# A decoder block on one core: the output projection ended row block by row block, the first up block put in another order, and the first chunk's operand sums written by transfers

## The chip, the core and the metric

The kernel runs on one core of a Trainium2 chip. The metric is the device time of one execution in microseconds (us). The engines are called as in the profile: PE (TensorE, matrix products), DVE (VectorE), ACT (ScalarE), POOL (GpSimd) and SP (SyncE, which only issues transfers here). POOL issues transfers too, the adding ones among them.

## The reference, cut to what matters

One decoder layer over 512 rows of width 2048, in float32. The parts that the change touches come after the two token mixers:

```python
y = jnp.concatenate([_rmsnorm(y_gm, gm_out_g[l]), _rmsnorm(y_lru, lru_out_g[l])], axis=-1)
x = x + jnp.einsum('bse,ed->bsd', y, w_out[l])            # output projection
h = _rmsnorm(x, norm2_g[l])
up = jnp.einsum('bsd,df->bsf', h, ffn_w_up[l])            # 2048 -> 2 * 6144
up = _causal_dwconv(up, ffn_conv_w[l], ffn_conv_b[l])     # width 3
gate, val = jnp.split(up, 2, axis=-1)
x = x + jnp.einsum('bsf,fd->bsd', jax.nn.gelu(gate) * val, ffn_w_down[l])
```

## The kernel before

**Products.** Every float32 operand is held as a rounded part and a rest (`h` and `l`); a product is three matmuls, h·h, h·l and l·h. `split` (L125) makes the pair: ACT casts (L126), DVE subtracts (L127). The up and down projections use Strassen's scheme in Winograd's form: an operand of 2x2 quarters gets seven slots, three of them quarters and four of them sums of quarters, and seven products replace eight. A unit (one weight operand against one activation operand) is 7 products of 6 matmuls (L854), in the order 1, 2, 6, 5, 3, 7, 4; `SLOTS` says which slots a product reads: products 1 and 2 read activation slots 6 and 4, products 6 and 5 slots 1 and 2, the rest 0, 3 and 5.

**Operands.** `stream` is the list in which operands are prepared: `Weights` and `Acts`, each with `load` (a transfer by SP, or transposes from rows), `sums` (three DVE instructions: L646 to L648 for weights, L672 to L674 for activations) and `pair` (the split). `prepare(upto)` writes these steps out in order: for each operand the load of the next, the sums of the next, its own pair, the load of the one after. For some weights ("made" ones: the first eight units and those around each chunk's start) the sums are made ahead in memory by adding transfers from POOL, spread over the kernel by `make` (L315), and `Weights.load` fetches them in place of the DVE sums. Raw operands lie in three rotating buffers `q` (a fourth is opened within the first down block), so a load waits for the pair of the operand three places before it. `ready(u)` says how far the list must be prepared before unit u.

**Stages around the change.** The output projection (`out_proj`, L556) runs over four column blocks d of 512 and, for each, over 8 steps of 128 in two halves, each half in two weight chunks; the four row blocks st of 128 rows have a bank of PSUM each and are taken in turn at every step, so that all four end together. Then DVE adds each to x (L569), `squares2` (L608) sends the rows to memory and squares them on ACT, `rms_rstd` (L224) makes the factor with 12 small DVE instructions for all rows, and `scale_rows` (L737) multiplies: column blocks 0 and 1 by DVE, 2 and 3 by ACT. From here on every engine's queue runs in the order in which the code writes it (L820). 40 idle products (L825) follow, then the first two activation operands: `from_rows` (L745) transposes two column tiles of 128 of x on PE into one bank (`tr`), ACT carries each into `q` (L753), and sums and pair follow. Operand m of the first up block holds column tiles 2m and 2m+1.

**Up blocks.** `up_block` (L882) runs 24 times (12 column groups, gate and value), 8 units each. In the first one the activations of the next units are transposed between the products: one tile when the operand is loaded, the other after the unit's third product. At the block's end `combine` (L867) makes the four output quarters from the seven banks, in one ACT copy and seven DVE instructions (L871 to L878); the next block's products take banks as these free them. After the first block the pools `tr` (1 bank) and `ps` (7 banks) are closed and one of 8 banks is opened. Convolution (L913, L918), gelu (L927), the product gate by value (L921) and the transfer to memory (`ad`, L923) are spread over the next block's units.

**Down blocks.** `down_block` (L947) reads `ad` back as activations, in chunks of 8, 8 and 6 operands; each chunk runs 4 blocks, one for each column block of the output. The operands of a chunk are spread in `stream` over the last units before it and its first units. At a block's end DVE and ACT carry the banks off (L971 to L978). A tail of plain products, `last_a` and `last_w`, ends the kernel.

Of the kernel before, what the change touches and what calls it, by code (L numbers as in the profile page):

```python
# [8 lines left out]
F32 = mybir.dt.float32  # L9
# [5 lines left out]
P = 128  # L15
# [63 lines left out]
def hybrid_block(ctx: ExitStack, tc: tile.TileContext, x, xT, w_in, w_out, w_up, w_dn, w_m4, w_dl, wab, wsT, vec, bs, vgb, fg, out):  # L79
# [235 lines left out]
    def make(n, after=None):  # L315
# [3 lines left out]
        for _ in range(min(n, len(to_make))):  # L319
            add, dst, src = to_make.pop(0)  # L320
            how = {"accum_op": ALU.add} if add else {}
            nc.gpsimd.dma_start(dst, src, max_dma_last_dim=8192, **how)  # L322
# [233 lines left out]
    def out_proj(d, half, ysrc, rstd, x_in, between=None):  # L556
        ps = [bank() for _ in range(NS)]
        for c in range(2):
            parts = wchunk(w_out[d, half * 2 + c])
            for i, wt in enumerate(parts):  # L560
                for kk in range(2):
                    e = c * 4 + i * 2 + kk
                    for st in range(NS):
                        mm3(ps[st], cols(ysrc[e], st), sl(wt, slice(None), kk, slice(None)), e == 0, e == NH - 1)
# [3 lines left out]
        for st in range(NS):  # L568
            nc.vector.scalar_tensor_tensor(x_in[:, st], ps[st], rstd[:, st:st + 1], x_in[:, st], ALU.mult, ALU.add)  # L569
# [38 lines left out]
    def squares2(d):  # L608
        nc.gpsimd.dma_start(x2d[d], x2[d])
        for st in range(NS):  # L610
# [46 lines left out]
    class Acts:  # L657


        def __init__(self, m, src=None, fill=None):  # L660
            self.m, self.src, self.fill = m, src, fill

        def load(self):
            self.q = slots("q")
            if self.fill is None:
# [4 lines left out]
        def sums(self):  # L670
            q = self.q
            nc.vector.tensor_tensor(q[:, 2:4], q[:, 7:8].broadcast_to([P, 2, 256]), q[:, 5:7], ALU.subtract)  # L672
            nc.vector.tensor_tensor(q[:, 1], q[:, 6], q[:, 2], ALU.subtract)
            nc.vector.tensor_tensor(q[:, 0], q[:, 4], q[:, 1], ALU.subtract)  # L674

# [61 lines left out]
    def scale_rows(d):  # L737
        for st in range(NS):
# [5 lines left out]

    def from_rows(m):  # L745

        def turn(q, kk):
            k = 2 * m + kk
            ps = pools["tr"].tile([P, S], F32, name="tr", tag="tr")
# [10 lines left out]
        def fill(q):  # L760
            turn(q, 0)
            halves.append(lambda: turn(q, 1))
# [7 lines left out]
    for c, s in zip(CHUNKS, starts):  # L770
        for i, p in enumerate(c):
            after.setdefault(s - 8 + spread[i] + 3, []).append(Acts(i, src=ad[p]))
# [29 lines left out]

    for d in range(4):
        if d == 3:
            prepare(place[2], place[2])
        out_proj(d, 0, ygm, rstd_g, x2[d], lambda c: squares2(d - 1) if d and c == 0 else None)
    squares2(3)
    rstd2 = const.tile([P, NS], F32, name="rstd2")
    rms_rstd(rstd2, ss2, D, NS)
    scale_rows(0)  # L810
# [13 lines left out]
    idle = pools["tr"].tile([P, S], F32, name="tr", tag="tr")  # L824
# [298 lines left out]
```

## Time and profile before

| | |
|---|---|
| time, median of 3 runs | 2063.87 us (2063.66 to 2065.06) |
| the profiled execution's own time | 2063.26 us |
| its span in the trace | 2061.6 us |
| PE, DVE, ACT, POOL busy | 2033.9, 1730.7, 904.3, 418.7 us |
| output projection ends, first product of the up blocks | 559.31, 574.28 us |
| first chunk's operands loaded | from 1514 us |

A row of a timeline gives the start, the duration, the engine, the line, what is written from what, and in brackets the idle time of that engine before the instruction with what ended it. A row of the table by stage gives the stretch, its length, each engine's busy time with the number of its instructions, the granted clock of PE (1.00 is full), the busy share of the transfer engines and what they moved in GB/s. Matmuls overlap, so their starts, not their durations, give the pace: 6669 in 800 us in an undisturbed stretch, or 0.120 us each. In a group of instructions the figures behind the bar are busy time, mean nanoseconds, and idle time before with its cause.

### The profile page before, as it was taken

How to read it: one execution, taken by the hardware profiler on the slowest of the kernel's cores; microseconds unless marked ns; L12 is line 12 of the kernel's file. 1: busy time of each engine (PE TensorE's matmuls, PEld its weight loads, DVE VectorE, ACT ScalarE, POOL GpSimd, SP SyncE). 2: the span in 40 equal slices, each digit the busy share in tenths (PEclk: the TensorE clock that was granted, in tenths of full speed). 3: DMA queues.
4: the chain of work that ended last, by engine and by line, in shares of the span. 5: the costliest groups of instructions: out<-in, count | busy, mean ns of one | idle time of the engine just before them, and what ended most of it. 6: DMA issues, size and time to landing. Idle time of an engine off the chain costs nothing.

```text
span 2061.6 us, 35459 instructions
## 1 busy us (share of the span) xinstructions
PE 2033.9 (99%) x14528; PEld 1920.2 (93%) x14528; DVE 1730.7 (84%) x2183; ACT 904.3 (44%) x887; POOL 418.7 (20%) x702
## 2 busy tenths in 40 slices
PE   9999999999989999999999999999999999999998
PEld 7888888888889999999999999999999999999996
DVE  7598882644379999999999999999989979879986
ACT  6445322423274444444444444444455345445443
POOL 0332233211222222222222222222211000000001
PEclk9999999999999999999999999999999999999999
DMA  7666687666435566656555655565556568558573
GB/s 244 185 170 165 176 208 178 179 188 203 139 120 161 164 160 177 172 154 179 167 156 172 167 169 172 161 172 159 154 206 214 189 224 277 184 196 285 175 245 138
DMA packets 105907, 376.39 MB, mean 183 GB/s; under 512 B 14608, under 2 KB 22160, under 8 KB 91792
## 3 DMA queue, kind: packets, MB, share of 16 engines
q1 hardware_dynamic: 65808, 246.30, 35.5%
q0 software_dynamic: 39360, 127.17, 25.6%
q8 instruction: 113, 1.85, 0.4%
q10 hardware_dynamic: 576, 0.66, 0.1%
q14 instruction: 50, 0.41, 0.1%
HBM read 341.57 MB, written 110.36 MB: 219 GB/s over the span
## 4 chain that ended last, share of the span: by engine, by line
PE 93%; DVE 4%; DMA 1%; ACT 1%; issue 0%; SPq 0%; DVEq 0%; ACTq 0%
PE qs L854 64%; PE ps L162 9%; PE ps L164 9%; PE ps L163 9%; DVE wl L127 1%; DMA q<-ad 1%; PE qs L163 1%; PE qs L164 1%; PE qs L162 1%; DVE al L127 1%; PE tr L751 0%; PE ps L582 0%; ACT wh L126 0%; DVE q L672 0%; DMA wraw<-w_in 0%
## 5 line engine op out<-in xcount | busy, mean ns | idle before, releaser
L854 PE MATMUL qs<-ah,wh 128*128 128x256 f32 x2688 | 762.7, 284 | 2.1 <-DVE pad L871 1.8
L854 PE MATMUL qs<-al,wh 128*128 128x256 f32 x2688 | 761.5, 283 | 0.0
L854 PE MATMUL qs<-ah,wl 128*128 128x256 f32 x2688 | 761.5, 283 | 0.0
L126 ACT CAST wh<-q 128x1792 fp32r<-128x1792 f32 (+1 forms) x282 | 476.7, 1691 | 640.1 <-PE qs L854 459.6
L127 DVE TENSOR_TENSOR wl<-q,wh 128x1792 fp32r<-128x1792 f32 (+1 forms) x282 | 567.7, 2013 | 54.2 <-ACT wh L126 53.6
L854 PEld LDWEIGHTS qs<-ah,wh 128*128 128x128 f32 x2688 | 516.8, 192 | 2.5 <-DVE pad L871 2.0
L854 PEld LDWEIGHTS qs<-al,wh 128*128 128x128 f32 x2688 | 516.8, 192 | 0.2 <-DVE al L127 0.2
L854 PEld LDWEIGHTS qs<-ah,wl 128*128 128x128 f32 x2688 | 516.8, 192 | 0.0
L854 PE MATMUL qs<-wh,ah 128*128 128x256 f32 x1232 | 350.4, 284 | 5.7 <-DVE xs L972 2.6
L854 PE MATMUL qs<-wl,ah 128*128 128x256 f32 x1232 | 349.8, 284 | 0.0
L854 PE MATMUL qs<-wh,al 128*128 128x256 f32 x1232 | 349.7, 284 | 0.0
L318 POOL COPY pace<-wl 128x1 f32<-128x1 f32 x236 | 125.8, 533 | 975.5 <-DVE wl L127 965.5
L127 DVE TENSOR_TENSOR wl<-wraw,wh 128x1024 fp32r<-128x1024 f32 (+2 forms) x105 | 117.9, 1125 | 150.6 <-ACT wh L126 145.7
L854 PEld LDWEIGHTS qs<-wh,ah 128*128 128x128 f32 x1232 | 237.6, 193 | 6.9 <-DVE xs L972 3.0
L854 PEld LDWEIGHTS qs<-wl,ah 128*128 128x128 f32 x1232 | 237.6, 193 | 0.1
L854 PEld LDWEIGHTS qs<-wh,al 128*128 128x128 f32 x1232 | 237.6, 193 | 0.0
L322 POOL DMA_DIRECT2D made<-w_m x324 | 232.1, 842 | 15.8 <-issue 15.7
L126 ACT CAST wh<-wraw 128x1024 fp32r<-128x1024 f32 (+2 forms) x105 | 102.1, 974 | 274.6 <-PE ps L163 142.6
L646 DVE TENSOR_TENSOR q<-q 128x512 f32<-128x512 f32 x226 | 154.5, 684 | 2.7 <-DMA q<-w_dn 2.6
L162 PE MATMUL ps<-xgh,wh 128*128 128x512 f32 x384 | 152.1, 397 | 0.7 <-ACT wh L126 0.7
L163 PE MATMUL ps<-xgl,wh 128*128 128x512 f32 x384 | 151.6, 395 | 0.0
L164 PE MATMUL ps<-xgh,wl 128*128 128x512 f32 x384 | 150.0, 395 | 0.0
(242 smaller groups left out, 2499.4 us busy)
## 6 DMA issues: line engine op xcount, KB each, us to landing
q<-w_up SPq DMA_DIRECT2D x176, 512.0 KB, 3.5
made<-w_m POOLq DMA_DIRECT2D x270, 256.0 KB, 5.0
wraw<-w_in SPq DMA_DIRECT2D x28, 1024.0 KB, 6.1
q<-made SPq DMA_DIRECT2D x54, 512.0 KB, 3.7
q<-w_dn SPq DMA_DIRECT2D x50, 512.0 KB, 3.6
wraw<-w_out SPq DMA_DIRECT2D x16, 1024.0 KB, 6.1
q<-w_dn SPq DMA_DIRECT2D x38, 384.0 KB, 4.5
ad<-gate POOLq DMA_DIRECT2D x48, 256.0 KB, 3.5
```

The costliest lines, as they stand in the source:

```text
L126: nc.scalar.copy(h, src)
L127: nc.vector.tensor_tensor(l, src, h.bitcast(F32), ALU.subtract)
L162: nc.tensor.matmul(ps, lhsT=ah, rhs=bh, start=start, stop=False)
L163: nc.tensor.matmul(ps, lhsT=ah, rhs=bl, start=False, stop=False)
L164: nc.tensor.matmul(ps, lhsT=al, rhs=bh, start=False, stop=stop)
L318: nc.gpsimd.tensor_copy(pace, after)
L322: nc.gpsimd.dma_start(dst, src, max_dma_last_dim=8192, **how)
L646: nc.vector.tensor_tensor(q[:, 2:4], q[:, 5:7], q[:, 7:8].broadcast_to([P, 2, 256]), ALU.add)
L854: nc.tensor.matmul(q[p][:, t], lhsT=x_, rhs=y_, start=first and t == 0 and n == 0, stop=last and t == 1 and n == 2, skip_group_check=True)
```

## The change

**The projection's end.** For the last column block (d = 3) the second weight chunk's steps are sorted by row block: a row block's four steps follow one another, and as it ends, `add(st)` and `norm2(st)` follow for it alone: squares on ACT, a square root on ACT, one reciprocal and four small DVE instructions, then `scale_rows` for column blocks 0 and 1 (block 1 of the last row block comes later). The sums of squares of column blocks 0 to 2 are added beforehand (`part2`), and `squares2(2)` moves ahead of that call.

**The first up block.** Idle products are 24, 8 and 8, in a bank of the other pool. Both column tiles of operands 0 and 1 are transposed at once, into two banks. Operand 0 is split in two pieces (`parts`): slots 4 to 6 need no sums. Later operands' transposes come after a unit's second and fifth product. At a block's last unit less is prepared ahead of `combine`, the rest after it; the down blocks likewise.

**The first chunk.** Its operands' sums are written to memory by 40 transfers from POOL, 5 for each of 8 operands, one at every second unit from the eleventh block on (`sum_up`). They can only add, so two quarters of each are stored negated (the gate product becomes two half instructions), and the signs are taken back where the banks are carried off (`plus`). Such an operand is loaded as 512 KB of sums and 384 KB of quarters in place of 512 KB, and has no DVE sums. The first chunk's `ad` is laid out quarter by quarter.

```diff
--- before.py
+++ after.py
@@ -312,12 +312,12 @@
...
-    def make(n, after=None):
+    def make(n, after=None, todo=to_make):
...
-        for _ in range(min(n, len(to_make))):
-            add, dst, src = to_make.pop(0)
+        for _ in range(min(n, len(todo))):
+            add, dst, src = todo.pop(0)
@@ -553,20 +553,30 @@
...
-    def out_proj(d, half, ysrc, rstd, x_in, between=None):
+    def out_proj(d, half, ysrc, rstd, x_in, between=None, in_turn=None):
...
+        def add(st):
+            nc.vector.scalar_tensor_tensor(x_in[:, st], ps[st], rstd[:, st:st + 1], x_in[:, st], ALU.mult, ALU.add)
...
-            for i, wt in enumerate(parts):
-                for kk in range(2):
-                    e = c * 4 + i * 2 + kk
-                    for st in range(NS):
-                        mm3(ps[st], cols(ysrc[e], st), sl(wt, slice(None), kk, slice(None)), e == 0, e == NH - 1)
+            todo = [(c * 4 + i * 2 + kk, sl(wt, slice(None), kk, slice(None)), st) for i, wt in enumerate(parts) for kk in range(2) for st in range(NS)]
+            turns = in_turn is not None and c == 1
+            if turns:
+                todo.sort(key=lambda t: t[2])
+            for e, w, st in todo:
+                mm3(ps[st], cols(ysrc[e], st), w, e == 0, e == NH - 1)
+                if turns and e == NH - 1:
+                    add(st)
+                    in_turn(st)
...
-        for st in range(NS):
-            nc.vector.scalar_tensor_tensor(x_in[:, st], ps[st], rstd[:, st:st + 1], x_in[:, st], ALU.mult, ALU.add)
+        if in_turn is None:
+            for st in range(NS):
+                add(st)
@@ -605,9 +615,14 @@
...
-    def squares2(d):
-        nc.gpsimd.dma_start(x2d[d], x2[d])
-        for st in range(NS):
+    ap, sums_of = ([tc.dram_tile([4, P, 256], F32, name=f"{n}{i}") for i in CHUNKS[0]] for n in ("ap", "as"))
+    for i in CHUNKS[0]:
+        ad[i] = ap[i].rearrange("s p c -> p s c")
+    def squares2(d, sts=range(NS)):
+        if NS - 1 in sts:
+            nc.gpsimd.dma_start(x2d[d], x2[d])
+        for st in sts:
@@ -657,21 +672,35 @@
...
-        def __init__(self, m, src=None, fill=None):
-            self.m, self.src, self.fill = m, src, fill
+        def __init__(self, m, src=None, fill=None, made=None):
+            self.m, self.src, self.fill, self.made = m, src, fill, made
...
-            if self.fill is None:
+            if self.made is not None:
+                nc.sync.dma_start(self.q[:, 0:4], self.made.rearrange("s p c -> p s c"))
+                nc.sync.dma_start(self.q[:, 4:7], self.src[:, 0:3])
+            elif self.fill is None:
...
+            if self.made is not None:
+                return
...
+        def parts(self):
+            act[self.m] = self.hl = act_tiles(self.m, [P, 7, 256])
+            (h, l), q = self.hl, self.q
+            nc.scalar.copy(h[:, 4:7], q[:, 4:7])
+            self.sums()
+            nc.vector.tensor_tensor(l[:, 4:7], q[:, 4:7], h[:, 4:7].bitcast(F32), ALU.subtract)
+            split(h[:, 0:4], l[:, 0:4], q[:, 0:4])
@@ -734,19 +763,23 @@
...
-    def scale_rows(d):
-        for st in range(NS):
+    def scale_rows(d, sts=range(NS)):
+        for st in sts:
...
+    def qbank():
+        return pools["ps"].tile([P, S], F32, name="qs", tag="qs")
...
-            ps = pools["tr"].tile([P, S], F32, name="tr", tag="tr")
+            ps = qbank() if m < 2 and kk else pools["tr"].tile([P, S], F32, name="tr", tag="tr")
@@ -758,8 +791,7 @@
...
-            turn(q, 0)
-            halves.append(lambda: turn(q, 1))
+            halves.extend((lambda: turn(q, 0), lambda: turn(q, 1)))
@@ -769,7 +801,7 @@
...
-            after.setdefault(s - 8 + spread[i] + 3, []).append(Acts(i, src=ad[p]))
+            after.setdefault(s - 8 + spread[i] + 3, []).append(Acts(i, src=ad[p], made=sums_of[i] if c is CHUNKS[0] else None))
@@ -800,14 +832,34 @@
...
+    rstd2 = const.tile([P, NS], F32, name="rstd2")
+    part2 = mx.tile([P, NS], F32, name="part2")
+    def norm2(st):
+        squares2(3, [st])
+        c = slice(st, st + 1)
+        v, y, u = (mx.tile([P, 1], F32, name=f"n2{n}", tag=f"n2{n}", bufs=2) for n in "vyu")
+        nc.vector.tensor_scalar(v, ss2[:, st, 3:4], 1.0 / D, part2[:, c], ALU.mult, ALU.add)
+        nc.scalar.activation(y, ss2[:, st, 3:4], AF.Sqrt, bias=part2[:, c], scale=1.0 / D)
+        nc.vector.reciprocal(y, y)
+        nc.vector.scalar_tensor_tensor(u, y, -0.5, y, ALU.mult, ALU.mult)
+        nc.vector.tensor_tensor(u, u, v, ALU.mult)
+        nc.vector.scalar_tensor_tensor(rstd2[:, c], u, 1.5, y, ALU.add, ALU.mult)
+        scale_rows(0, [st])
+        if st < NS - 1:
+            scale_rows(1, [st])
...
-        out_proj(d, 0, ygm, rstd_g, x2[d], lambda c: squares2(d - 1) if d and c == 0 else None)
-    squares2(3)
-    rstd2 = const.tile([P, NS], F32, name="rstd2")
-    rms_rstd(rstd2, ss2, D, NS)
-    scale_rows(0)
+        if d == 3:
+            with tc.high_priority(offset=AHEAD):
+                squares2(2)
+                nc.vector.tensor_reduce(part2, ss2[:, :, 0:3], mybir.AxisListType.X, ALU.add)
+                nc.vector.tensor_scalar(part2, part2, 1.0 / D, RMS_EPS, ALU.mult, ALU.add)
+        out_proj(d, 0, ygm, rstd_g, x2[d], lambda c: squares2(d - 1) if d in (1, 2) and c == 0 else None, norm2 if d == 3 else None)
@@ -821,25 +873,27 @@
...
-    idle = pools["tr"].tile([P, S], F32, name="tr", tag="tr")
-    for _ in range(40):
-        nc.tensor.matmul(idle[:, 0:256], lhsT=stream[0].hl[0][:, 0, 0:P], rhs=stream[0].hl[0][:, 1], start=True, stop=True)
+    idle = qbank()
+    def idle_products(n):
+        for _ in range(n):
+            nc.tensor.matmul(idle[:, 0:256], lhsT=stream[0].hl[0][:, 0, 0:P], rhs=stream[0].hl[0][:, 1], start=True, stop=True)
...
+    idle_products(24)
...
-    stream[first].sums()
-    scale_rows(1)
-    stream[first].pair()
+    idle_products(8)
+    stream[first].parts()
+    scale_rows(1, [NS - 1])
...
+    idle_products(8)
...
-    def qbank():
-        return pools["ps"].tile([P, S], F32, name="qs", tag="qs")
@@ -882,11 +936,13 @@
...
-            prepare(ready(u0 + m))
-            for p in ORDER:
+            prepare(ready(u0 + m) if m < 7 else min(ready(u0 + m), place[u0 + m + (2 if u0 else 1)]))
+            for n, p in enumerate(ORDER):
...
-                if p == 6:
-                    rest_of_loads()
+                if n in (1, 4) and halves:
+                    halves.pop(0)()
+            if u0 >= 80 and m % 2:
+                make(1, todo=sum_up)
@@ -897,6 +953,7 @@
...
+        prepare(ready(u0 + 7))
@@ -918,7 +975,12 @@
...
-                nc.vector.tensor_tensor(gate, gate, dst, ALU.mult)
+                if 2 * g + n in CHUNKS[0]:
+                    for t in (slice(0, 256), slice(256, 512)):
+                        nc.vector.scalar_tensor_tensor(gate[:, t], gate[:, t], -1.0 if (t.start == 0) == (j == 1) else 1.0, dst[:, t], ALU.mult, ALU.mult)
+                else:
+                    nc.vector.tensor_tensor(gate, gate, dst, ALU.mult)
@@ -936,6 +998,19 @@
...
+    sum_up = []
+    for k in range(len(CHUNKS[0]) + 3):
+        for r in range(4):
+            if 0 <= k - r < len(CHUNKS[0]):
+                dst, src = (t.rearrange("s (a b) c -> s a (b c)", b=8) for t in (sums_of[k - r], ap[k - r]))
+                sum_up += [
+                    [(0, dst[0:2], src[0:3:2]), (0, dst[2:4], src[1:3])],
+                    [(1, dst, src[3:4].broadcast_to([4, 16, 2048]))],
+                    [(1, dst[0:2], src[1:2].broadcast_to([2, 16, 2048]))],
+                    [(1, dst[0], src[2])],
+                ][r]
@@ -949,7 +1024,8 @@
...
-            prepare(ready(u0 + m))
+            ends = m == size - 1 and u0 + m + 3 < len(units)
+            prepare(min(ready(u0 + m), place[u0 + m + 2]) if ends else ready(u0 + m))
@@ -965,23 +1041,25 @@
...
+        plus = ALU.subtract if ci == 0 else ALU.add
...
-        tt(X11, X11, q[2], ALU.add)
+        tt(X11, X11, q[2], plus)
...
-        tt(X12, X12, q[3], ALU.add)
+        tt(X12, X12, q[3], plus)
...
-            lambda: tt(c5, c5, c6, ALU.add),
+            lambda: tt(c5, c6, c5, plus),
...
-            lambda: tt(c6, c6, c7, ALU.add),
+            lambda: tt(c6, c6, c7, plus),
...
-            lambda: tt(c5, c5, c7, ALU.add),
+            lambda: tt(c5, c5, c7, plus),
@@ -990,6 +1068,7 @@
...
+        prepare(ready(u0 + size - 1))
...
```

## The prediction

> **What bounds the kernel now.** I read the table by stage first, then PE's own idle times, then what the other engines do at those places.
>
> ```profile
> span 2061.6 us, 35459 instructions
> 700.00:1500.00 800.00, 800.00 (x6669) 800.00 (x6668) 766.72 (x973) 361.72 (x299) 207.84 (x357) 1.00 0.59 166
> 1500.00:1640.00 140.00, 135.40 (x1101) 0.98 0.61 211
> 1960.00:1990.00 30.00, 28.85 (x241) 1.00 0.58 192
> 574.60:578.40 3.80, 3.80 (x20) 3.80 (x19) 1.96 (x3) 2.27 (x2) 0.00 (x0) 0.50 0.54 197
> ```
>
> In the long middle PE never waits: 6669 matmuls in 800 us, 8.336 per us, 0.120 us each. There only fewer matmuls would help, and the change removes none. DVE is at 766.72 of 800 us (96%), so it bounds wherever it gets more work. At 1500 to 1640, 1101 matmuls need 132.1 us: 7.9 us are lost. At 1960 to 1990 it is 1.1 us. At 574.6 the clock is at half.
>
> PE's timeline at these places:
>
> ```profile
> 558.69 0.39 PE L163 MATMUL ps<-wl,ygmh 128*128 128x512 f32 x1
> 558.92 0.39 PE L164 MATMUL ps<-wh,ygml 128*128 128x512 f32 x1
> 559.47 5.06 PE L826 MATMUL tr<-wh 128*128 128x256 f32 x40 [0.16 <-DVE x L569]
> 571.62 1.11 PE L751 MATMUL tr<-ident,x 128*128 128x128 f32 x4 [3.35 <-ACT q L753]
> 574.28 0.56 PE L854 MATMUL qs<-ah,wh 128*128 128x256 f32 x1
> 586.38 0.66 PE L751 MATMUL tr<-ident,x 128*128 128x128 f32 x4 [1.77 <-ACT q L753]
> 600.19 0.65 PE L751 MATMUL tr<-ident,x 128*128 128x128 f32 x4 [1.78 <-ACT q L753]
> 628.39 0.39 PE L854 MATMUL qs<-ah,wh 128*128 128x256 f32 x1 [1.82 <-DVE pad L871]
> 631.87 0.36 PE L854 MATMUL qs<-ah,wh 128*128 128x256 f32 x1 [0.30 <-DVE v L877]
> 1558.98 0.58 PE L854 MATMUL qs<-wh,ah 128*128 128x256 f32 x1 [2.40 <-ACT c L870]
> 1607.01 0.39 PE L854 MATMUL qs<-wh,ah 128*128 128x256 f32 x1 [1.45 <-DVE xs L972]
> 1981.38 0.38 PE L854 MATMUL qs<-wh,ah 128*128 128x256 f32 x1 [1.15 <-DVE xs L972]
> ```
>
> Between the projection's end (559.31) and the first product (574.28) lie 15 us with 16 useful transposes, at most 0.66 us for four by the rows below 574.28. After the 3.35 us wait the clock is halved; it was halved after the wait of 2.40 us too, not after 1.82. The second up block's first unit has 12 matmuls left at 631.87 and ends at 633.3; I use that mark below.
>
> **The change, part by part.**
>
> *From the projection to the first product.* What sets it now, on DVE and ACT:
>
> ```profile
> 544.17 1.23 DVE L127 TENSOR_TENSOR wl<-wraw,wh 128x1024 fp32r<-128x1024 f32 x1 [4.17 <-ACT wh L126]
> 557.31 2.79 DVE L569 SCALAR_TENSOR_TENSOR x<-ps,rstd_g,x 128x512 f32<-128x512 f32 x4 [11.91 <-PE ps L164]
> 560.95 0.17 DVE L229 TENSOR_REDUCE rms_v<-ss 128x4 f32<-128x16 f32 x1 [0.85 <-ACT sq L612]
> 563.35 1.67 DVE L741 TENSOR_SCALAR x<-x,rstd 128x512 f32<-128x512 f32 x4
> 566.88 0.69 ACT L753 ACTIVATE q<-tr,vc 128x512 f32<-128x512 f32 x1 [0.75 <-PE tr L751]
> 567.60 0.69 DVE L672 TENSOR_TENSOR q<-q 128x512 f32<-128x512 f32 x1 [2.58 <-ACT q L753]
> 571.02 2.02 DVE L127 TENSOR_TENSOR al<-q,ah 128x1792 fp32r<-128x1792 f32 x1 [0.22 <-ACT ah L126]
> 583.20 2.55 ACT L743 ACTIVATE x<-x,rstd 128x512 f32<-128x512 f32 x4
> 618.61 2.02 DVE L127 TENSOR_TENSOR al<-q,ah 128x1792 fp32r<-128x1792 f32 x1
> 2023.04 1.28 ACT L1040 ACT_TABLE_LOAD   x1
> 2054.07 0.30 ACT L1040 ACTIVATE r3y<-ss,part 128x1 f32<-128x1 f32 x1
> 2054.99 0.16 DVE L1045 SCALAR_TENSOR_TENSOR r3r<-r3u,r3y 128x1 f32<-128x1 f32 x1
> ```
>
> Sorted steps need both halves of the last weights at once. They are ready at 545.4, and the last chunk (48 matmuls of 0.23 us, the step from 558.69 to 558.92) starts at 548.4: covered by 3 us, else up to 3 us would show. A row block now takes 2.7 us of PE and some 2.5 us of DVE (add 0.75, five small ones of 0.16 to 0.2, two scalings of 0.42), so only the last shows. The square root brings a table load of 1.28 us, and the next gelu another; ACT is 45% busy there and hides both. The new root's chain stands at the kernel's end: 1.1 us from the root's start (2054.07) to the factor (2055.15).
>
> Last row block: added at 560.1, squared at 560.95, factor at 562.1, scaled at 562.5 (now 565.0). If its add queues behind the scalings of the block before, all this is 0.8 us later. I take half. The 24 idle products (0.127 us each) start between 559.4 and 561.0, as their bank is or isn't the one that the last add reads; with the add, at 560.2, they end at 563.2. Eight transposes one after another, some 0.11 us each: 564.1. The second tile carried into `q`: 565.2. Sums (1.54 us): 566.8. The rests of slots 4 to 6, three sevenths of 2.02 us: 567.7. First product at 567.8, 6.5 us earlier. PE's waits on this way are under 1 us, so the clock stays, which saves 2.0 us (some 20 matmuls at 0.21). Together 8.5 us.
>
> *The first block gives part back.* I walked the queues instruction by instruction with these durations. The old order gives 632.1 for the mark at 633.3, without the half clock, and waits of 1.9 where the profile has 1.77 and 1.78. In the new order a unit's second transpose, after the fifth product, waits for ACT, which carried nothing off while it scaled column blocks 2 and 3 (2.55 us after a cast): 1.3 us in unit 0, 1.9 in units 1 and 3. DVE, whose sums begin only 2.4 us earlier (565.2 against 567.6), ends the last activation's rest at 615.7, where 618.61 + 2.02 = 620.6 stands now; PE waits 2.0 us for it. The second block's second product waits 2.1 us for `combine`, since `idle` and the two early tiles have turned the banks and it now gets one that the sixth step frees; one weight pair less ahead of `combine` is what keeps this near the 1.82 + 0.30 of now. The mark falls at 627.9, or 628.7 with the late add: **-5.0 us**. At worst DVE's start decides alone, -2.4; at best no new wait appears, -8.5.
>
> The 1.9 to 2.1 us waits lie between the 1.82 that left the clock alone and the 2.40 that halved it; one half-clock stretch is some 30 matmuls at 0.21 instead of 0.12, 2.7 us. The Trainium skill (TensorE: Matmul & The Clock Gate, "What's actually happening") has the clock throttled after an idle window of about 3.4 us, counted in fixed windows. By that rule none of the new waits would cost it, and the sum would stay; the trace's 2.40 us does not agree, so I keep the risk.
>
> *Half instructions for the gate product.*
>
> ```profile
> L921 DVE TENSOR_TENSOR gate<-gate,cv 128x512 f32<-128x512 f32 x6 | 4.2, 692 | 0.2
> L918 DVE SCALAR_TENSOR_TENSOR gate<-pad,vc,gate 128x512 f32<-128x512 f32 x8 | 6.0, 748 | 0.1
> L674 DVE TENSOR_TENSOR q<-q 128x256 f32<-128x256 f32 x8 | 3.4, 425 | 0.3
> 708.60 0.68 DVE L871 TENSOR_TENSOR pad<-c,qs 128x512 f32<-128x512 f32 x1
> ```
>
> Two halves of some 0.44 us for one of 0.69: 0.19 us more, 16 times, in four value blocks. In the block that ends at 708.9, DVE reaches `combine` just in time, and the first bank that would be late has some 0.6 us left; 0.76 us more makes 0.2 us of wait. **+0.6 us** (0 to 3.0, all of it on the path).
>
> *The 40 transfers.* 11.3 MB written, issued on POOL, which is 26% busy; what queues behind them is `made` and `ad`, not due soon. Two steps of one operand lie at least four calls, 40 us, apart, so none waits for the one before. Weight loads take longer beside them, but have room: 0 here, a rival below.
>
> *The first chunk.*
>
> ```profile
> L672 DVE TENSOR_TENSOR q<-q 128x512 f32<-128x512 f32 x8 | 5.5, 688 | 3.0 <-DMA q<-ad 3.0
> 1548.93 0.32 SPq L639 DMA_DIRECT2D q<-made  x1
> 1553.89 1.69 ACT L126 CAST wh<-q 128x1792 fp32r<-128x1792 f32 x1 [0.93 <-DMA q<-w_dn]
> 1560.51 0.68 DVE L871 TENSOR_TENSOR pad<-c,qs 128x512 f32<-128x512 f32 x1
> 1605.48 0.68 DVE L971 TENSOR_TENSOR xs<-xs,qs 128x512 f32<-128x512 f32 x1
> ```
>
> DVE is late at 1560.51, the last up block's `combine`, and at 1605.48, the first down block's end; all 7.9 us follow from these two and the half clock between. Removed: 8 x (0.688 + 2 x 0.425) = 12.3 us of DVE, five of the eight before 1560; and one activation pair (1.94 us) moves behind `combine`. That `combine` comes early enough then. But the load now has 896 KB, like the weights whose cast starts 4.96 us after their issue. With three buffers each operand takes a third of landing 5.0 + cast 1.7 + rest 2.0 + 0.2, 2.97 us, where PE uses one in 2.92 (19 operands in 11 units of 5.04): the loads become as tight as DVE was, and the first down block's end stays late, with PE there sooner. The same walk loses 9.2 us in the old order (the profile: 7.9) and 2.1, 2.9 or 4.7 with landings of 4.6, 5.2 or 5.8 us. I take 2.8 left: **-5.1 us** (-3 to -7).
>
> [...]
>
> *The down blocks' ends.* Before 1981.38 DVE makes the tail's activation pair (2.3 us) ahead of L971; now it follows: **-1.1 us** (0 to -1.1).
>
> Sum: -5.0 + 0.6 - 5.1 - 1.1 = -10.6 us on the profiled execution's 2063.26 (its span of 2061.6 and 1.7 around it), so 2052.7. It lies 0.6 below the median, to which the same saving gives **2053.3 us**.
>
> **The rivals.**
>
> *Both places are freed less.* DVE's start alone decides the first block (-2.4), the loads land in 5.8 us (-3.2), and 1.5 comes from the gate halves: -2.4 - 3.2 - 1.1 + 1.5 = -5.2, 2058.7. For it: DVE at 96%. Against: the walk meets today's marks within some 1.2 us.
>
> *The waits move, no net change.* As that, and the new 2 us waits halve the clock once (+2.7): -2.5, 2061.4. For it: 2.40 did so. Against: 1.82 did not.
>
> *All of it comes through.* No new wait, the loads hide: -8.5 - 7.9 - 1.1 = -17.5, 2046.4. Against: ACT's scalings stand where they did.
>
> *Slower: the 40 transfers starve the weight loads.*
>
> ```profile
> q<-w_up SPq DMA_DIRECT2D x176, 512.0 KB, 3.5
> made<-w_m POOLq DMA_DIRECT2D x270, 256.0 KB, 5.0
> ```
>
> Between about 980 and 1380 us, a buffer comes round in 3 x 5.04 = 15.1 us, of which sums, cast and rest take 5.2 and the landing 3.5: 6.4 us of room. Where landings pass 9.9 us, each microsecond above costs one in three units, 27 us over 80 units. At 10.5 us: +16, less the 10.6 saved, 2069.3. Against: 270 similar transfers run now at 3.5, with the transfer engines at 0.60.
>
> **How the numbers follow.** The forecast, 2050 to 2057: 0.55. Both freed less: 0.17. No net change: 0.12. All of it: 0.10. Slower: 0.06. A measurement of this kernel tells 0.2%, 4.1 us, from no change: faster is below 2059.7 (forecast, less, all: 0.83 with a little of the next), same 0.11, slower 0.06. The range 2047 to 2061 leaves out the outer half of "all of it", half of "no net change" and "slower".
>
> **What would show it.** Right: the first product near 568 at full clock, two waits near 1.9 us for L753 in the first block, one at the second block's start, no `L672` rows near 1520 to 1585, no wait at 1550 to 1560, some wait left near 1600 for L972, none near 1970. Wrong: a first product after 571, a granted clock of 0.50 in the first block, landings of the first chunk's loads far from 5 us, waits at the ends of the second to eighth value blocks, or a PE that waits between 980 and 1380.

## The result, and the profile after

The changed kernel takes 2124.31 us (2120.85 to 2126.71) beside 2064.47 us (2063.66 to 2065.28) for the kernel before, measured together: a ratio of 1.029, 95% interval 1.0277 to 1.0303. It is 60 us slower; the forecast was 2053.3 us. The profiled execution has a span of 2123.5 us, 61.9 more than before.

Lines of the code have moved: `product` is L908 (L854 before), the weights' three sums L661 to L663 (L646 to L648), the load of an up weight L652 (L637), `combine` L925 to L932 (L871 to L878), the projection's add L561 (L569), the load of an activation's sums L681. First the stages, PE alone: the stretch, its length, PE's busy time with its matmuls, the granted clock, the transfer engines' share, GB/s. The kernel after:

```profile
640.00:1000.00 360.00, 360.00 (x3002) 1.00 0.59 166
1000.00:1460.00 460.00, 418.53 (x3312) 0.95 0.64 170
1520.00:1760.00 240.00, 234.09 (x1937) 1.00 0.65 211
2020.00:2050.00 30.00, 30.00 (x253) 1.00 0.59 191
```

and the kernel before in the stretches that answer to the second and third of these:

```profile
1000.00:1460.00 460.00, 460.00 (x3836) 1.00 0.61 169
1460.00:1700.00 240.00, 235.40 (x1934) 0.99 0.60 198
```

An undisturbed stretch has 8.336 matmuls per us. From 1000 to 1460 the kernel after has 3312 in place of 3836: 524 fewer, or 62.9 us, in a stage that lost nothing before. All else is small: the first chunk has 1937 matmuls where it had 1934 (7.6 us lost in place of 8.0), the down blocks' wait of 1.1 us is gone (x253 in 30 us). Who waits for whom in that stage (us in total, times, longest), first DVE, then PE:

```profile
DVE q L661 <- DMA q<-w_up: 66.8, 21, 6.4
PE qs L908 <- DVE pad L925: 26.8, 9, 6.9
PE qs L908 <- DVE wl L127: 13.7, 7, 2.8
```

Before, DVE waited for no weight load there. Now 21 of them come late, DVE waits 66.8 us for them, and PE 41.4 us for DVE. The rest of the 62.9 us, 21.5, fits the half clock behind these waits: it was 0.50 after the one of 4.12 us below, and its mean over the stage is 0.95, which is some 23 us of 460. The chain of waits tells the same for the whole span (the first line of before, the second of after):

```profile
PE 93%; DVE 4%; DMA 1%; ACT 1%; issue 0%; SPq 0%; DVEq 0%; ACTq 0%
```

```profile
PE 69%; DVE 17%; DMA 11%; issue 2%; ACT 2%; SPq 0%; DVEq 0%; ACTq 0%; POOL 0%
```

One such case in the timeline of after, with the transfer that it meets:

```profile
1239.82 1.28 POOL L322 DMA_DIRECT2D as<-ap  x1
1243.58 0.33 SPq L652 DMA_DIRECT2D q<-w_up  x1
...
1246.92 1.53 DVE L975 SCALAR_TENSOR_TENSOR gate<-pad,vc,gate 128x512 f32<-128x512 f32 x2
1254.73 0.69 DVE L661 TENSOR_TENSOR q<-q 128x512 f32<-128x512 f32 x1 [6.28 <-DMA q<-w_up]
...
1268.95 0.58 PE L908 MATMUL qs<-ah,wh 128*128 128x256 f32 x1 [4.12 <-DVE pad L925]
```

A 512 KB transfer of the new kind is issued at 1239.82, a weight load at 1243.58. DVE is free for the load at 1248.45 (1246.92 + 1.53), gets it 6.28 us later, and PE pays 4.12 us at the block's end, where `combine` comes late. The landings in that stage, after (from 990 to 1460 us) and then before (from 990 to 1400):

```profile
q<-w_up SPq DMA_DIRECT2D x80, 512.0 KB, 5.2
as<-ap POOLq DMA_DIRECT2D x24, 256.0 KB, 9.6
as<-ap POOLq DMA_DIRECT2D x8, 512.0 KB, 15.9
as<-ap POOLq DMA_DIRECT2D x8, 128.0 KB, 5.6
```

```profile
q<-w_up SPq DMA_DIRECT2D x81, 512.0 KB, 3.5
```

The transfer engines are not full: their share is 0.64, 0.61 before. And 512 KB take three times as long as 128 KB, although a weight load of 512 KB landed in 3.5 us. So it is not the bytes alone. The new transfers that are slow have an access pattern of their own: 2 or 4 slots outside and 16 rows of 8 KB inside. 24 of the 40 have it. The 16 copies of 256 KB show the difference within one run: eight of them have it and land in 7.8 to 11.0 us; the two slots of the other eight lie end to end in memory, and these land in 4.0 to 6.0 us. For each of the eight transfers of 512 KB the adding packets of 8 KB (at least 0.60 us, most take 0.629) that run at once were counted from the packets of the trace: over the transfer's time the median is 4, where the core has 16 transfer engines. (Adding packets of the weights' sums are in the count, as the trace doesn't tell them apart.)

### The profile page after: what moved, and what is told of

Read it like the earlier page. It is cut to its first block, busy times and chain, and to the rows that moved or that the text cites. A ratio compares the mean times of both kernels' runs of the same rounds, so it can differ in the third digit from the quotient of the medians.

```text
span 2123.5 us, 35520 instructions
## 1 busy us (share of the span) xinstructions
PE 2054.3 (97%) x14528; PEld 1934.5 (91%) x14528; DVE 1724.2 (81%) x2186; ACT 909.5 (43%) x894; POOL 444.9 (21%) x742
## 4 chain that ended last, share of the span: by engine, by line
PE 69%; DVE 17%; DMA 11%; issue 2%; ACT 2%; SPq 0%; DVEq 0%; ACTq 0%; POOL 0%
PE qs L908 41%; DMA q<-w_up 9%; PE ps L164 9%; PE ps L162 8%; PE ps L163 8%; DVE wl L127 7%; DVE q L661 2%; DVE q L662 1%; DVE al L127 1%; DMA q<-w_dn 1%; DVE gate L975 1%; DMA q<-ap 1%; DVE cv L975 1%; ACT wh L126 1%; PE qs L163 1%
## 5 line engine op out<-in xcount | busy, mean ns | idle before, releaser
L908 PE MATMUL qs<-ah,wh 128*128 128x256 f32 x2688 | 771.6, 287 | 29.0 <-DVE pad L925 26.8
L908 PE MATMUL qs<-ah,wl 128*128 128x256 f32 x2688 | 769.4, 286 | 13.7 <-DVE wl L127 13.7
L908 PE MATMUL qs<-al,wh 128*128 128x256 f32 x2688 | 768.7, 286 | 2.9 <-DVE al L127 2.4
L127 DVE TENSOR_TENSOR wl<-q,wh 128x1792 fp32r<-128x1792 f32 (+1 forms) x282 | 567.9, 2014 | 58.2 <-ACT wh L126 58.0
L908 PEld LDWEIGHTS qs<-ah,wh 128*128 128x128 f32 x2688 | 524.4, 195 | 32.1 <-DVE pad L925 28.9
L908 PEld LDWEIGHTS qs<-ah,wl 128*128 128x128 f32 x2688 | 524.1, 195 | 15.2 <-DVE wl L127 15.1
L908 PEld LDWEIGHTS qs<-al,wh 128*128 128x128 f32 x2688 | 524.4, 195 | 3.3 <-DVE al L127 2.6
L908 PE MATMUL qs<-wl,ah 128*128 128x256 f32 x1232 | 349.1, 283 | 3.9 <-DVE wl L127 3.9
L908 PE MATMUL qs<-wh,ah 128*128 128x256 f32 x1232 | 349.0, 283 | 2.0 <-DVE xs L1050 1.7
L908 PE MATMUL qs<-wh,al 128*128 128x256 f32 x1232 | 348.6, 283 | 0.0
L318 POOL COPY pace<-wl 128x1 f32<-128x1 f32 x236 | 115.4, 489 | 995.9 <-DVE wl L127 985.8
L127 DVE TENSOR_TENSOR wl<-wraw,wh 128x1024 fp32r<-128x1024 f32 (+2 forms) x105 | 118.1, 1127 | 151.8 <-ACT wh L126 146.8
L908 PEld LDWEIGHTS qs<-wl,ah 128*128 128x128 f32 x1232 | 236.5, 192 | 4.7 <-DVE wl L127 4.7
L908 PEld LDWEIGHTS qs<-wh,ah 128*128 128x128 f32 x1232 | 236.4, 192 | 2.6 <-DVE xs L1050 1.9
L908 PEld LDWEIGHTS qs<-wh,al 128*128 128x128 f32 x1232 | 236.5, 192 | 0.0
L322 POOL DMA_DIRECT2D made<-w_m x324 | 232.0, 836 | 18.4 <-issue 16.5
L661 DVE TENSOR_TENSOR q<-q 128x512 f32<-128x512 f32 x226 | 154.8, 685 | 68.9 <-DMA q<-w_up 67.2
```

The costliest lines, as they stand in the source:

```text
L127: nc.vector.tensor_tensor(l, src, h.bitcast(F32), ALU.subtract)
L318: nc.gpsimd.tensor_copy(pace, after)
L661: nc.vector.tensor_tensor(q[:, 2:4], q[:, 5:7], q[:, 7:8].broadcast_to([P, 2, 256]), ALU.add)
L908: nc.tensor.matmul(q[p][:, t], lhsT=x_, rhs=y_, start=first and t == 0 and n == 0, stop=last and t == 1 and n == 2, skip_group_check=True)
```

## The experiments

**Theory 1:** each outer index of a transfer goes to one transfer engine, so that it runs as 16 slow packets behind one another on 2 or 4 engines, and a weight load, which has rows on all 16, waits for these. **Theory 2:** the adding transfers are simply too much traffic.

*The axes in the other order.*

```diff
-dst, src = (t.rearrange("s (a b) c -> s a (b c)", b=8) for t in (sums_of[k - r], ap[k - r]))
+dst, src = (t.rearrange("s (a b) c -> a s (b c)", b=8) for t in (sums_of[k - r], ap[k - r]))
...
-[(1, dst, src[3:4].broadcast_to([4, 16, 2048]))],
+[(1, dst, src[:, 3:4].broadcast_to([16, 4, 2048]))],
```

and so for the other four of each operand.

> The 40 transfers with their axes in the other order: the 16 rows outside, the 2 or 4 slots inside; the same bytes, number, places and results. Theory 1 (each outer index of a transfer goes to one transfer engine, so that a transfer of 4 x 16 rows runs as 16 packets of 0.63 us behind one another on 4 engines, some 10 us, and a weight load that has rows on those engines lands behind it): the loads of the up weights between 1000 and 1440 land as before the change, median 3.3 to 3.8 us, maximum under 8; PE loses 0 to 5 us there in place of 62.7, and the time is 2124.3 - 62.7 + (0 to 5) = 2061.6 to 2066.6 us. Theory 2 (the 11.3 MB of adding transfers are too much beside the loads, however they are spread): median 5 us or more, 50 us or more lost, 2110 to 2125.

Measured: 2066.1 us (ratio 1.0005, 0.9997 to 1.0014). Its stage, its waits of DVE, its landings:

```profile
1000.00:1460.00 460.00, 458.65 (x3817) 1.00 0.73 192
```

```profile
DVE q L661 <- DMA q<-w_up: 4.2, 6, 1.6
```

```profile
q<-w_up SPq DMA_DIRECT2D x93, 512.0 KB, 3.7
as<-ap POOLq DMA_DIRECT2D x24, 256.0 KB, 5.2
as<-ap POOLq DMA_DIRECT2D x8, 512.0 KB, 7.2
```

The same bytes by as many transfers, at a higher share of the engines (0.73), and 2.3 us are lost (19 matmuls) in place of 62.9. The 512 KB transfers land in 7.2 us and not 15.9, and the median of the adding packets that run at once, counted the same way, is 10 to 16 in place of 4. Theory 2 falls.

*The transfers left out.*

```diff
-made=sums_of[i] if c is CHUNKS[0] else None
+made=ap[i] if c is CHUNKS[0] else None
...
+    sum_up.clear()
```

> The 40 transfers are left out, and the first chunk's loads read the four stored parts where the sums would stand: as many bytes and loads, but the sums of the first chunk's operands are left out of the result. Both theories of the transfers (few engines, or too many bytes): no loss between 1000 and 1460, 2124.3 - 62.7 = 2061.6 us (2060 to 2063), and the first chunk keeps its loss of 7.6 us, as its loads alone set that. If the halves of the gate product or the finer stores made the loss: above 2100. If the transfers also disturbed the first chunk: below 2058.

Measured: 2062.45 us (ratio 0.9985, 0.9976 to 0.9994), 460.00 of 460 us busy in the stage. All 60 us come from the transfers; the gate product's halves and the finer stores cost nothing in that stage.

*Copies in place of adding.*

```diff
-[(1, dst, src[3:4].broadcast_to([4, 16, 2048]))],
+[(0, dst, src[3:4].broadcast_to([4, 16, 2048]))],
```

and so for the two other adding ones.

> The 40 transfers at the same places, with the same rows on the same axes, but all are plain copies: the adding is left out, so the sums of the first chunk's operands are left out of the result. Theory 1 (16 packets behind one another on 2 or 4 engines): a copy's packet takes 0.31 us and not 0.63, so an engine is held 5 us and not 10; a load then lands at 3.5 + 5.0 = 8.5 us at most, under the 9.9 that stop PE: 0 to 10 us lost, 2062 to 2072 us. Theory 2 (the transfers' total work): an operand's packets take 512 x 0.31 + 896 x 0.31 where they took 512 x 0.31 + 896 x 0.63, 0.60 of it, so about 38 us of the 62.7 stay: 2090 to 2105.

Measured: 2084.3 us (1.0093, 1.0079 to 1.0106): between the two ranges. The stage, DVE's waits in it, and the landings of the largest transfers:

```profile
1000.00:1460.00 460.00, 443.98 (x3633) 0.99 0.65 185
```

```profile
DVE q L661 <- DMA q<-w_up: 29.0, 18, 3.8
```

```profile
as<-ap POOLq DMA_DIRECT2D x8, 512.0 KB, 10.5
```

The loss is 24 us (203 matmuls), although no load landed later than 9.5 us, below the 9.9 that my forecast took for the limit. So the limit was wrong, and this run by itself decides between neither theory. From the traces I took each weight load's landing and whether DVE waited for it: with this kernel the shortest landing that DVE waited for is 6.3 us, with the change 6.4, with the other order of the axes 5.4. In the kernel before, the first sum starts 1.9 us (median) after the landing. The room is some 2 us, not 6.4. A second size was off too: 16 packets of 0.31 us and the 3.5 of a load had made me expect a load's landing of 8.5 us at most, and the latest took 9.5; the 512 KB copies themselves land after 10.5.

*One kind alone on few engines.* From the run with the axes changed, the one transfer that adds to all four slots is put back:

```diff
-[(1, dst, src[:, 3:4].broadcast_to([16, 4, 2048]))],
+[(1, *(t.rearrange("a s c -> s a c") for t in (dst, src[:, 3:4].broadcast_to([16, 4, 2048]))))],
```

> As the run with the 16 rows outside (2066.1 us), but the one transfer of each operand that adds its last part to all four sums has its 4 slots outside again, as in the change: 8 transfers of 512 KB stay on 4 engines, 32 are spread. Theory (each adding transfer on few engines costs by itself: the change had 16 of them and VectorE waited 66.8 us for loads, 4.2 each): 8 x 4.2 = 33 us of waits of VectorE beside the 4 of the spread run, of which, as in the change (62.7 lost of 66.8), nearly all reaches the end: 2066 + 25 to 33 = 2091 to 2099 us. Rival (the loss came from three kinds of transfers of one or several operands piling up on the same engines): under 10 us more, 2066 to 2076.

Measured: 2097.5 us (1.0157, 1.0128 to 1.0187), within the theory's 2091 to 2099, DVE waiting 38.2 us for 12 loads. The stage, and the landings of the eight transfers:

```profile
1000.00:1460.00 460.00, 433.39 (x3520) 0.97 0.67 180
```

```profile
as<-ap POOLq DMA_DIRECT2D x8, 512.0 KB, 15.8
```

The stage loses 37.9 us (316 matmuls), so eight transfers make more than half of the loss; no pile-up of several kinds is needed.

*The first chunk as before.* No transfers, sums on DVE, parts in the old layout; the projection, the first block and the block ends stay changed.

```diff
-Acts(i, src=ad[p], made=sums_of[i] if c is CHUNKS[0] else None)
+Acts(i, src=ad[p])
...
-if 2 * g + n in CHUNKS[0]:
+if False:
...
-plus = ALU.subtract if ci == 0 else ALU.add
+plus = ALU.add
```

> The first chunk as before the change (sums on VectorE, parts stored in the old layout, one gate product, no transfers); the projection by row blocks, the rearranged first up block and the later weight pairs at the ends of blocks stay. Theory: 3.75 us saved at the first block and 1.1 at the down blocks' ends, so 2064.5 - 4.9 = 2059.6 us (2058 to 2061), with the first chunk's loss at 7 to 8 us as before. Rival: the pair that now goes behind the last up block's end frees VectorE in time there too, and some 3 to 4 us of the first chunk's loss go: 2055.5 to 2057. Rival: the saving at the first block doesn't reach the end: 2063 to 2065.

Measured: 2064.9 us (1.0002, 0.9993 to 1.0011), no gain where 4.9 us were due; the first chunk's stretch lost 11.4 us (x1906 from 1460 to 1700). Part of what was missing was already lost when the output projection ended, after as many matmuls as before. Its last two:

```profile
560.95 0.39 PE L163 MATMUL ps<-wl,ygmh 128*128 128x512 f32 x1
561.17 0.39 PE L164 MATMUL ps<-wh,ygml 128*128 128x512 f32 x1
```

This is the kernel after; before, the last one started at 558.92. Up to the last weight chunk, some 12 us before, the matmuls are the same in the same order, and in the changed kernels so far those from 12 to 385 us follow each other after 0.2328 us on average, not 0.2311 (gaps of over 0.3 us left out). What differs by the code is an address: seven new tiles of 32 bytes per partition move the projections' weight tiles by 224 bytes. Unused tiles test it:

```diff
 part2 = mx.tile([P, NS], F32, name="part2")
+mx.tile([P, 8], F32, name="spare")
```

> As the run with the 16 rows outside, and one unused tile of 32 bytes per partition more beside the new small tiles of the norm. The change put 7 x 32 = 224 bytes there and so moved the projections' weight tiles by 224 bytes; with 32 more they stand 256 bytes from their old places. Theory (the place of the weight tiles sets the time of a projection matmul: 0.2328 us on average from 12 to 385 us in the changed kernels, 0.2311 before, with the same instructions in the same order): the mean goes back to 0.2311 and the time from 2066.1 to 2063.8 us (2063.0 to 2064.6). Rival (the longer program or chance makes the 2.3 us until 470 us): 2065.5 to 2066.7.

```diff
+for i in range(7):
+    mx.tile([P, 8], F32, name=f"spare{i}")
```

> The kernel before with seven unused tiles of 32 bytes beside the norm's small tiles, and nothing else changed: the projections' weight tiles move by 224 bytes, to where they stand in the changed kernel. Theory (place of the weight tiles): 0.2328 us for a projection matmul in place of 0.2311, 2064.8 + 2.3 = 2067.1 us (2066.3 to 2068). Rival (program length or chance): 2064 to 2065.5.

Measured: 2062.1 us (0.9992, 0.9983 to 1.0001) in place of 2066.1, and 2067.2 us (1.0014, 1.0005 to 1.0023) for the kernel before; the mean of a projection matmul goes back to 0.2311 us in the first and to 0.2328 in the second, to the last digit. The theory of the place holds; the first time came out 1.7 us lower than it has it. Then the kernel before with other distances, each with one time only (`mx.tile([P, 16]...)` for 64 bytes, and so on):

> The kernel before with one unused tile of 32 bytes per partition beside the norm's small tiles, so that the projections' weight tiles start 32 bytes lower, at a multiple of 64 bytes. If the place within 64 bytes decides (it was 32 bytes into a 64-byte line at 0.2311 us per projection matmul, and 0 at 0.2328): 0.2328 and about 2.3 us more. If the place within 128 or 256 bytes decides: some third value, or 0.2311.

> As before_32 with 64 bytes. If the place within 64 bytes decides: 0.2311 us per projection matmul and the time of before. If within 128 or 256: another value, 0.2328 perhaps.

> As before_32 with 128 bytes. If the place within 64 or 128 bytes decides: 0.2311 us per projection matmul. If within 256: another value.

Measured: 2065.6, 2056.3 and 2062.3 us, beside 2064.8. The stretch from 12 to 385 us of the kernel before, of the one with 64 bytes and of the one with 224:

```profile
12.00:385.00 373.00, 373.00 (x1614) 1.00 0.69 184
```

```profile
12.00:385.00 373.00, 373.00 (x1672) 1.00 0.70 187
```

```profile
12.00:385.00 373.00, 373.00 (x1602) 1.00 0.68 183
```

With 32, 128 and 256 bytes it is 1606, 1624 and 1613. No rule by 64 or 128 bytes holds; 256 bytes give the value of 0 again.

*4 KB rows for the first chunk.* With the 32 bytes; stores, sums and loads lie as 128 rows of 4 x 256.

```diff
-ap, sums_of = ([tc.dram_tile([4, P, 256], F32, name=f"{n}{i}") for i in CHUNKS[0]] for n in ("ap", "as"))
+sums_of = [tc.dram_tile([P, 4, 256], F32, name=f"as{i}") for i in CHUNKS[0]]
...
-dst, src = (t.rearrange("s (a b) c -> s a (b c)", b=8) for t in (sums_of[k - r], ap[k - r]))
+dst, src = sums_of[k - r], ad[k - r]
...
+[(1, dst, src[:, 3:4].broadcast_to([P, 4, 256]))],
...
```

> As the run before the last (32 bytes more), and the first chunk's stored parts and sums lie as before the change and as the weights' sums do, 128 rows of 4 x 256, so that a load takes one row of 4 KB and one of 3 KB per partition in place of 7 of 1 KB; the 40 transfers work on 128 rows of 1 to 4 KB. Theory (the landings of the first chunk's 1 KB rows, 4.5 to 5.8 us, set its 9 us of loss): landings of 3.6 to 4.7 us, 2 to 4 us lost between 1460 and 1700 in place of 9.3, 2063.8 - 6 = 2058 us (2056 to 2060). Rival 1 (the transfers, now up to 1408 small packets for each operand in place of 176, hold up the loads between 1000 and 1400): 5 to 20 us lost there, 2063 to 2078. Rival 2 (the loads are not what sets the first chunk): 2063 to 2064.5.

Measured: 2070.4 us (1.0035, 1.0022 to 1.0047). The first rival came true, and the theory only in its direction:

```profile
1000.00:1460.00 460.00, 451.19 (x3710) 0.99 0.74 187
1460.00:1700.00 240.00, 236.81 (x1966) 1.00 0.65 210
```

The loads of the first chunk's sums land in 3.5 us, the parts in 4.1, and the first chunk's stretch loses 4.2 us in place of 6.1 (x1950 in the run with the 32 bytes alone): the rows are worth 2 us there, and the rest of what the theory would have them save, from 9.3, had come with the 32 bytes already. But the transfers in small rows lose 15 us between 1000 and 1460, where the run with the 32 bytes alone loses 5.4 (x3791).

*What is worth keeping.*

```diff
-prepare(ready(u0 + m) if m < 7 else min(
+prepare(ready(u0 + m) if m < 7 or u0 else min(
```

added to the run with the first chunk as before, with the 32 bytes:

> As the run with the first chunk as before (no transfers, sums on VectorE), with the 32 bytes more, and the weight pairs at the ends of the second to last up block again ahead of the block's end, as before the change; the first up block and the down blocks' ends stay changed. Theory (in the run without this, 11.4 us were lost between 1460 and 1700 and 7.9 before, since the pair that waits behind the last up block's end makes weights late): 7.9 us lost there again, and 2064.8 - 3.75 (first block) - 1.1 (down blocks' ends) = 2060 us (2059 to 2061). Rival (that pair's place has no part in it): 11 us lost, 2064.9 - 2.3 = 2062.6 us (2062 to 2063.5).

Measured: 2058.1 us (0.9969, 0.9958 to 0.9981), faster than both kernels. On the point that it tested it is inconclusive: the stretch of the first chunk loses 10.2 us (x1916), between the 7.9 and the 11 of the two theories; the kernel before alone loses 7.0 to 9.2 there in the runs with other distances, and the same version with 96 bytes, below, 7.8 (x1936). Last, the forecast's sum without the transfers and with the weights in their old rest by 256 bytes, and the two versions with 64 bytes (96 in place of 32):

> As the run without the 40 transfers (the sums of the first chunk's operands are left out of the result), with the 32 bytes more that put the projections' weight tiles 256 bytes from their old places. What is left is the forecast's sum without the term of the transfers. If its other terms hold: 2064.5 - 10.6 = 2053.9 us (2051.5 to 2056). If, as the profiles so far say, the first chunk's term is worth 2 us (6 lost in place of 7.9) and the first block 4 to 5: 2064.5 - 4.5 - 2 - 1.1 = 2056.9 us (2056 to 2059). If the first chunk is worth nothing: 2059 to 2060.5.

> As the run that keeps the first up block and the down blocks' ends and leaves the first chunk as before, with 96 bytes in place of 32, so that the projections' weight tiles start 320 = 256 + 64 bytes lower than before. Theory (the place counts modulo 256 bytes, and 64 bytes lower a projection matmul takes 0.2230 us and not 0.2311): the projections end some 9 us earlier, 2058.1 - 9 = 2049 us (2047.5 to 2051). Rival (the effect needs the exact place, not its rest by 256): 2057 to 2062.

> The whole change with the 16 rows outside and the 96 bytes. Theory: 2062.1 - 9 = 2053 us (2051 to 2055), behind the run with the first chunk as before (2049), as the spread transfers still cost 2 to 5 us between 1000 and 1460 and the first chunk gains no more than that. Rival (the first chunk's sums in memory pay after all): at or below 2049.

Measured: 2057.35 us (0.9968, 0.9958 to 0.9979), 2049.9 us (0.9933, 0.9921 to 0.9946) and 2052.5 us (0.9944, 0.9932 to 0.9957), the last two as expected. The first block with the first chunk as before is the fastest; the whole change with spread transfers is 2.7 us behind it, with 7 us lost in the stage of the transfers (x3776).

## Why the prediction was wrong

**The 40 transfers: the step that failed.** I put them at "0 here", with a rival of 0.06, and they cost 62.9 us from 1000 to 1460. Two things in that step were wrong, the landings and the room, and its price with them. *The landings:* I compared them with `made`, "270 similar transfers" at 5.0 us. They are not similar: `made` is issued as 32 or 128 rows with no slots outside them; 24 of the 40 have 2 or 4 slots outside, and these 24 land in 7.8 to 16.5 us. The order of the axes makes this, as the first experiment shows; that an outer index is tied to one engine is a reading of the 4 and the 10 to 16 packets at once, since the trace names no engine. The Trainium skill (DMA: Bandwidth & Descriptors, "Why a DMA increments its semaphore by 16 and not by 1") has this rule: the number of engines is the largest up to 16 that divides the slowest dimension of both sides. By it 4 x 16 rows run on 4 engines and 16 x 4 on 16; the counted 4, and 10 to 16, fit it. The rule speaks against this change, and I had not weighed it. *The room:* I worked out 6.4 us from a buffer's round of 15.1 us. But DVE, 96% busy, does its work in a fixed order: in the case above it came to the load 4.9 us after its issue, 1.4 behind the usual 3.5. Time that the buffer has left lies behind the sums and helps a late landing nothing. *The price:* my rival took one late unit in three, each 0.6 us over the limit. The number was not too low (21 of 80 loads came late), but each cost DVE 3.2 us, 66.8 in all, as the limit lay lower; and DVE, with 1.7 us to spare in a block of 40 (4% of it), hands nearly all of it on. With the latest landings, 11 to 12 us, in place of its 10.5, the rival's own rate would have said 30 to 57 us.

**Projection to first block: right, and 1.2 us short in size.** The first product starts 8.7 us after the start of the projection's last matmul (569.86 less 561.17), before 15.4: 6.7 us earlier, forecast 6.5. As bounded, the last add was late, behind the scalings of the block before. The clock stayed full, and the waits came where the walk had them:

```profile
563.23 3.13 PE L880 MATMUL qs<-wh 128*128 128x256 f32 x24 [1.67 <-DVE x L561]
569.86 0.28 PE L908 MATMUL qs<-ah,wh 128*128 128x256 f32 x1
576.44 0.66 PE L784 MATMUL tr<-ident,x 128*128 128x128 f32 x4 [1.41 <-ACT q L786]
584.33 0.66 PE L784 MATMUL tr<-ident,x 128*128 128x128 f32 x4 [1.77 <-ACT q L786]
598.13 0.66 PE L784 MATMUL tr<-ident,x 128*128 128x128 f32 x4 [1.78 <-ACT q L786]
619.61 0.58 PE L908 MATMUL qs<-al,wh 128*128 128x256 f32 x1 [2.39 <-DVE al L127]
628.19 0.39 PE L908 MATMUL qs<-ah,wh 128*128 128x256 f32 x1 [0.64 <-DVE pad L932]
631.76 0.28 PE L908 MATMUL qs<-ah,wl 128*128 128x256 f32 x1
```

The 378th matmul of the up blocks, the last of the second block's first unit, starts at 631.76, 70.6 us after the projection's last matmul; before it was 74.35. That is -3.8 for the -5.0. In the kernels with the 32 bytes it is -4.4 to -5.0. The wait for L127 was put at 2.0 and measured 2.39, and it halved the clock (0.56 granted from 619.6 to 623.0 us), the risk of 2.7 us that I had named; the one at the second block's start was put at 2.1 and measured 0.64.

**Gate halves: +0.6 forecast, 0 measured** (360 of 360 us busy from 640 on; 460 of 460 from 1000 on without the transfers). It lay within the bounds.

**The first chunk: right in kind, mis-sized.** -5.1 was forecast (2.8 us left); -0.4 came (7.6 left). The wait at the last `combine` is gone, as forecast, and the loads took DVE's place, as the walk said they might: PE waits 3.9 us for L127 there and 1.7 at the first down block's end. ACT's waits, after:

```profile
ACT ah L126 <- DMA q<-ap: 12.8, 7, 3.4
ACT wh L126 <- DMA q<-w_dn: 12.4, 7, 5.4
```

The term that was off is the landing: I took 5.0 us for the whole of a load, and the last part of an operand alone took 4.9 at the median, of the weights 5.4. The chunk's 1 KB rows are one reason: with 4 KB rows these are 4.1 and 5.1, and 4.2 us are lost in place of 6.1. Still, 8.0 less 4.2 would not have been 5.1.

**The down blocks' ends: right**, -1.1, as the row from 2020 to 2050 shows.

**A term that I didn't have:** +2.25 us up to the projection's end, by the place of the weight tiles, if that is what the unused tiles change.

Sum: 2.25 - 3.8 + 62.9 - 0.4 - 1.1 = 59.9 of the 61.9 us; another 1.1 us is lost between 1460 and 1520 (491 matmuls for 500), just behind the last transfers, and 0.9 us stays unassigned. Without the transfers and that place the gain is 6.6 us (4.3 to 8.7) where 10.6 were forecast: by the profile 4.75 at the first block, 2.2 at the first chunk (x1952), 1.1 at the down blocks' ends.

## What to carry to other kernels

Before pricing a transfer by a row of "similar" ones, compare the access patterns: sizes and queue were alike here, and the order of two axes was worth 58 us. The room of a prefetch is the time until its first consumer comes round in that engine's own order, not the time its buffer has to spare; on an engine that is 96% busy nearly all lateness is handed on (62.9 of 66.8 us here). And a new small tile can move large ones: compare a stage that the change doesn't touch before trusting a difference of 2 us.

## What the hardware showed unexpectedly

**A few bytes of unused tiles change the pace of a matmul.** Per projection matmul (128x512, f32), by how many bytes lower the code puts the weight tiles: 0 or 256: 0.2311 us; 32: 0.2321; 64: 0.2230; 128: 0.2297; 224: 0.2328. From 0 to 64 bytes that ends the projections 9.35 us earlier (549.57 for 558.92), and the best version took nearly the same gain (2058.1 to 2049.9). That the weights' place does it is read from the code: the same bytes move some other tiles on that side of the memory too, and no run moves the weights alone. Why the pace depends on an address is not settled.

**The length of a wait alone doesn't decide on the clock.** A wait of PE of 2.31 us in the fastest version left the clock full, one of 1.86 us in the run with the axes changed and 32 bytes halved it. The fastest version's row of the timeline, and its stretch behind the wait with the granted clock:

```profile
608.20 0.39 PE L907 MATMUL qs<-al,wh 128*128 128x256 f32 x1 [2.31 <-DVE al L127]
```

```profile
608.10:611.00 2.90, 2.81 (x23) 1.00 0.57 188
```

and the other:

```profile
1353.58 0.39 PE L909 MATMUL qs<-ah,wh 128*128 128x256 f32 x1 [1.86 <-DVE pad L926]
```

```profile
1353.60:1356.50 2.90, 2.90 (x15) 0.57 0.79 224
```

The Trainium skill (TensorE: Matmul & The Clock Gate, "What's actually happening") has windows that run freely and do not start with the wait. That two waits of different length end the wrong way round agrees with it; its length of about 3.4 us for an idle window does not, as 1.86 us were enough here.
